# A merged instruction order, with one matmul cadence in the scheduler's clock instead of two

## The chip, the cores and the metric

The kernel runs on one core of a Trainium2 chip. The metric is the device time of one execution in microseconds (us); lower is better. Of several executions the median is given. Engines are named as the profile names them: PE (TensorE, matrix multiply), PEld (its weight loads), DVE (VectorE), ACT (ScalarE), POOL (GpSimd), SP (SyncE, which here issues all DMAs). Each engine takes its instructions strictly in the order in which the program lists them.

## The reference

One decoder layer over 576 tokens: 512 of a prompt and 8 sequences of 8 sample tokens. What is computed, cut to its core:

```
proj = rmsnorm(x, norm1_g) @ w_in                     # -> qkv_a, z, beta, a, q_b, k_b, v_b
qkv_a = silu(short_conv(qkv_a))                       # mixer A: gated DeltaNet, 4 heads of 128
lmat  = strict_lower((kb @ k.T) * decay); a_mat = lmat + I
u, w  = triangular_solve(a_mat, vb), triangular_solve(a_mat, kb * exp(G))
S     = scan over chunks;  oa = rmsnorm(o) * silu(z)
ob    = dilated_mixture(q_b, k_all, v_all)            # mixer B: 8 heads of 64, sample tokens
                                                      # attend to a cache of 1024 past tokens
h1 = x + concat(oa, ob) @ w_o
y  = h1 + square(relu(rmsnorm(h1) @ w_up)) @ w_down   # 1024 -> 4096 -> 1024
```

Outputs are y, the new keys and values, the DeltaNet states and the last convolution rows.

## The kernel before

Tokens stand on the free axis, 576 columns, in two halves of 288. A weight product is made in three matmuls: each factor is split into a high part (type fp32r, by ACT) and a low part (the rest, by DVE or POOL), and high by high, high by low and low by high are summed in PSUM. The stages are: `proj_a` (q, k and v of mixer B; tiles `pa`, 260 or 512 columns a matmul; weight chunks `wq`, `wk`, `wv`), `proj_b` (everything of mixer A; tiles `pg`, 288 columns; chunks `wb`), the prompt's attention in 16 units (`sc`, `ptp`, `pv`), the sample tokens' attention (`s`, `os`, `pts`, `ocT`; its cached keys and values come in 48 DMAs of 512 KB into `kv` and `morekv`), the triangular solve (`sub_prompt`), the DeltaNet chain (`py`, `pu`, `cha`, `chb`, `cs`, `sn`), the output projection `proj_o` (first its attention half, `pg<-mob`, then its DeltaNet half, `pg<-moa`) and the feed-forward stage `mlp_gemm` (2904 matmuls of 288 columns, tiles `pg<-xf` and `pg<-hid`).

No order is written by hand. Each stage is a set of generators ("tasks") that queue their operations; the class `Flow` (L72 on) merges them while the kernel is built. For every engine it keeps a rough clock `free[engine]`; each operation has a cost in ns; at each step the task whose next operation can start soonest (plus a bias of its kind) is issued, and the engine's clock moves on by the cost. Tasks added with `fill=True` (`proj_a`, `proj_b`, `proj_o`, `mlp_gemm`) take PE whenever nothing else is ready on it. So the costs decide, for every engine at once, where an operation that waits for another engine stands among the filling matmuls; nothing of this clock exists when the program runs.

The cost of a matmul is given by `mm` (L257): the number of columns divided by 2.4, plus 3 ns, plus `extra`. The feed-forward stage passes `extra=8` (in `three` and in its call of `gemm`), all others nothing.

Three places matter further on:

- The zero fill (`zero_fill`, L1155): 25 us into the planner's clock POOL sets a tile `zero`, and SP writes it to the scratch `dU` in DRAM: 2064 rows of 129 floats, 1032 KB. Around it stand the loads of the chunks `wk`, which the k group of `proj_a` needs.
- The sums of squares of x: ACT squares (`sq<-xr`), POOL adds (`acc<-acc,sq`, seven times), PE sums over partitions (`ssum`), DVE forms the variance, POOL takes the power (`rs`), and PE broadcasts it (`rowb`).
- The triangular solve: 15 pairs of small steps on DVE (`sub<-sub`), a few DMAs between SBUF places, then eight pairs of a product and a sum (`pr<-sub`, `sub<-pr`), then DMAs through `dU` into `silvz`, on which PE's first product of the chain (`py<-silvz,big`) waits. After the last matmul of `proj_b` PE makes the transposes `pvt`, `pss`, `pk`, `pq`, whose results DVE and ACT take out of PSUM, and what else is ready, up to that `py`.

Of the kernel before, what the change touches and what calls it, by code (L numbers as in the profile page):

```python
# [11 lines left out]
F32R = mybir.dt.float32r  # L12
# [200 lines left out]
def hymba_step(ctx: ExitStack, tc: tile.TileContext, a):  # L213
# [14 lines left out]
    def get(use, shape, name, dt=F32):  # L228
        k = home[use]
        free = lambda: live[use] < cap[use] and live[k] < cap[k]  # L230
        while not free():
            yield free
        live[use] += 1
        live[k] += 1
        return pools[k].tile(shape, dt, name=name, tag=k, bufs=cap[k])

    def rel(*uses):
        def go():
            for u in uses:
                live[u] -= 1  # L240
                live[home[u]] -= 1
        fl.do(go)
# [5 lines left out]
    def size(x):  # L248
        n = 1
        for q in x.shape[1:]:  # L250
            n *= q
        return n
# [1 line left out]
    on_psum = lambda x: x.tensor.space == PSUM  # L254
    ap = lambda x: not isinstance(x, (int, float))

    def mm(out, lhsT, rhs, start, stop, share=1, extra=0):  # L257
        n = size(rhs) * (1 if rhs.dtype == F32R else 4)
        cost = max(n, size(lhsT) * (1 if rhs.dtype == F32R else 4)) / 2.4 + 3 + extra
        cost = cost if share == 1 else cost / share + 15  # L260
        fl.op("PE", (cost, n / share * lhsT.shape[0] / 128),
              lambda: nc.tensor.matmul(out, lhsT, rhs, start=start, stop=stop, skip_group_check=True))  # L262
# [230 lines left out]
    def weights(g, k):  # L493
        if (g, k) not in wready:
            yield lambda: (g, k) in wready
        w, t = wready.pop((g, k))
        fl.at(t + 200)
        return w
# [58 lines left out]
    def warm_up():  # L557


        act(warm, zeros[:, :1])  # L560
        p = yield from get("x", [128, 128], "warm")
        for _ in range(WARM):
            mm(p, zeros, zeros, True, True)
        rel("x", "k")
# [36 lines left out]
    def token_sums(src):  # L601
        p = yield from get("x", [128, 5], "ssum")
        for t, (o, n) in enumerate(TT):
            mm(p[:n, t:t + 1], src[:, o:o + n], ones[:, 0:1], True, True)
        yield 0
        return p
# [396 lines left out]
    sil = {}  # L1003
    UW = 604

    def gemm(wh, wl, x_h, x_l, nk, stride, off, after, extra=0):


        for hf, (c0, c1) in enumerate(HALF):
            p = yield from get("g", [128, 288], "pg")  # L1010
            for j in range(nk):
                s = slice(j * stride + off, j * stride + off + 128)
                mm(p, wh[:, s], x_h[:, j, c0:c1], j == 0, False, extra=extra)
                mm(p, wh[:, s], x_l[:, j, c0:c1], False, False, extra=extra)
                mm(p, wl[:, s], x_h[:, j, c0:c1], False, j == nk - 1, extra=extra)
                yield 0
            fl.spawn(after(hf, p))

# [651 lines left out]
    high = lambda t, j, n=1: t[:, j * 288:(j + n) * 288]  # L1670
    low = lambda t, j, n=1: t[:, (j + 8) * 288:(j + 8 + n) * 288]
# [89 lines left out]
    hid, Q, read = {}, {}, {}  # L1761
# [8 lines left out]
    def three(p, w, c, x, j, first, last):  # L1770
        c = slice(c * 128, c * 128 + 128)
        l = w[:, 512:]
        mm(p, w[:, c], high(x, j), first, False, extra=8)
        mm(p, w[:, c], low(x, j), False, False, extra=8)
        mm(p, l[:, c], high(x, j), False, last, extra=8)

    def up_classical(u):

        fl.spawn(up_square(u))
        w, P = {}, {}  # L1780
        for i in range(4):
            for hf in range(2):
                for r in range(2):
                    if not i:
                        P[hf, r] = yield from get("g", [128, 288], "pg")
                    for k in range(2):
                        if (r, k) not in w:
                            w[r, k] = yield from weights(("u", u), f"A{r + 1}{k + 1}")
                        j = 2 * hf + k
                        yield from factor(("x", i), j)  # L1790
                        three(P[hf, r], w[r, k], i, xf[i], j, i == 0 and k == 0, i == 3 and k == 1)
                        yield 0
        for hf in range(2):
            for r in range(2):
                fl.spawn(up_relu(u, hf, r, P[hf, r]))
        rel("mw", "mw", "mw", "mw")
# [6 lines left out]
    def up(u):  # L1803
        fl.spawn(up_square(u))
        A = yield from get("g", [128, 288], "pg")
        for p in PO:
            w = yield from weights(("u", u), p)
            if p in (2, 5):
                B = yield from get("g", [128, 288], "pg")
            if p in (6, 7, 3, 4):  # L1810
                yield from seen(("u", u, {6: 1, 7: 6, 4: 7, 3: 5}[p]))
            P = B if p in (2, 5, 3) else A
            for i in range(4):
                j = OF_X[p]
                yield from factor(("x", i), j)
                three(P, w, i, xf[i], j, i == 0 and p in (1, 2, 5), i == 3)
                yield 0
            rel("mw")
            fl.spawn(up_out(u, p, P), "out")
# [59 lines left out]
    def add_down(m, hf, p, last):  # L1879
        c0, c1 = HALF[hf]  # L1880
        tt(h1[m][:, c0:c1], p, h1[m][:, c0:c1], OP.add)
        rel("g")
        if last:
            yield 0
            dma(a["yT"][:, m, c0:c1], h1[m][:, c0:c1])
        yield 0

    def mlp_gemm():
        yield lambda: "proj_o" in done
        for g in order:  # L1890
            if g[0] == "d":
                c, i = g[1:]
                wh, wl = yield from weights(g, 0)
                if not i:
                    yield lambda: all(("hid", 2 * c + q, hf) in done for q in range(2) for hf in range(2))
                for j in range(2):
                    after = lambda hf, p, m=2 * i + j: add_down(m, hf, p, c == 7)
                    yield from gemm(wh, wl, hid[c][:, 0], hid[c][:, 1], 4, 256, j * 128, after, extra=8)
                rel("mw", "mw")
                if i == 3:  # L1900
                    rel("big")
                continue
            if g[1] % 2 == 0:
                hid[g[1] // 2] = yield from get("big", [128, 2, 4, NT], "hid", F32R)
            if g[1] < CLASSICAL:
                yield from up_classical(g[1])
            else:
                yield from up(g[1])
            if g == ("u", 15):
                rel("big", "big", "big", "big")  # L1910
# [36 lines left out]
    fl.add(proj_o(), "fill", True)  # L1947
    fl.add(stats2())
    fl.add(mlp_gemm(), "fill", True)
    fl.run()  # L1950

# [89 lines left out]
```

## Time and profile before

| what | value |
|---|---|
| median of 3 runs | 818.16 us (816.64 to 821.53) |
| the profiled execution | 818.95 us, its span 817.2 us |
| PE busy | 792.2 us, 97% of the span |
| DVE busy | 568.7 us, 70% |
| ACT busy | 348.3 us, 43% |
| POOL busy | 109.4 us, 13% |
| feed-forward stage, the last piece of the chain of waits | 370.65 us, 2794 matmuls recorded |

Busy time counts an instruction from its start to its end, and neighbouring matmuls overlap; a PE that starts its matmuls late still reads as busy as long as a gap stays below the length of one matmul (some 290 ns). A timeline row gives the start, the time it covers, the operation as `output<-inputs`, how many were merged, and in brackets how long the engine sat idle before it and what ended that.

### The profile page before, as it was taken

The page shows a single profiled execution, that of the slowest core. Times are in us where ns is not written, and L with a number is a line of the kernel's source. Part 1 is how long each engine was busy: PE and PEld are TensorE (multiplying, and loading weights), DVE is VectorE, ACT ScalarE, POOL GpSimd, SP SyncE. Part 2 cuts the span into 40 slices and gives each one's busy share as a digit, 9 for nine tenths or more (in the row PEclk, how much of TensorE's full clock was granted, in tenths as well). Part 3 has the DMA queues.
Part 4 walks back from the last instruction along what each step waited for, and adds up shares of the span by engine and source line. Part 5 has one row for each costly group of instructions (what it writes and reads, how often), then busy time and mean ns, then how long its engine had stood idle before and what let it go on. Part 6 is the DMA issues. An engine that isn't in the chain of part 4 may idle for free.

```text
span 817.2 us, 15699 instructions
## 1 busy us (share of the span) xinstructions
PE 792.2 (97%) x6323; PEld 728.1 (89%) x6323; DVE 568.7 (70%) x1250; ACT 348.3 (43%) x728; POOL 109.4 (13%) x128
## 2 busy tenths in 40 slices
PE   8989998999999999999997999999999999999998
PEld 8968877879778687778997999999999999999998
DVE  4366269888776785668798886768677676867642
ACT  5547453655242134443466543515343351534400
POOL 3443224134224000121000000000000000000000
PEclk9999999999999999999999999999999999999999
DMA  7732320106686799122221141404123130412302
GB/s 270 125 112 77 123 68 31 55 27 245 211 345 185 273 319 327 49 93 81 104 104 52 59 150 52 129 27 155 53 94 113 52 129 27 155 53 95 112 30 87
DMA packets 49864, 99.05 MB, mean 121 GB/s; under 512 B 12864, under 2 KB 26304, under 8 KB 49792
## 3 DMA queue, kind: packets, MB, share of 16 engines
q1 hardware_dynamic: 49792, 98.05, 36.6%
q8 instruction: 50, 0.82, 0.4%
q14 instruction: 22, 0.18, 0.1%
HBM read 88.15 MB, written 9.69 MB: 120 GB/s over the span
## 4 chain that ended last, share of the span: by engine, by line
PE 73%; issue 9%; DVE 7%; DMA 6%; ACT 2%; SPq 2%; POOL 1%; POOLq 0%; ACTq 0%; DVEq 0%
PE pg L262 53%; PE pa L262 7%; DVE y L285 2%; SPq L321 2%; PE cha L262 2%; DMA wr<-in_wk_dram 2%; DMA morekv<-in_cv_dram 1%; PE os L262 1%; PE ptp L265 1%; DMA morekv<-in_ck_dram 1%; PE cs L262 1%; DMA silvz<-dU 1%; PE sc L262 1%; PE s L262 1%; PE sn L262 1%
## 5 line engine op out<-in xcount | busy, mean ns | idle before, releaser
L262 PE MATMUL pg<-hid,mw 128*128 128x288 f32 x1536 | 204.7, 295 | 0.0
L262 PEld LDWEIGHTS pg<-hid,mw 128*128 128x128 f32 x1536 | 203.9, 188 | 0.0
L262 PE MATMUL pg<-xf,mw 128*128 128x288 f32 x1368 | 186.0, 297 | 4.6 <-ACT xf L270 3.8
L262 PEld LDWEIGHTS pg<-xf,mw 128*128 128x128 f32 x1368 | 183.7, 189 | 5.6 <-ACT xf L270 4.3
L278 DVE TENSOR_TENSOR h<-pg,h 128x288 f32<-128x288 f32 x160 | 72.5, 455 | 94.6 <-PE pg L262 93.8
L270 ACT ACTIVATE mw<-wr 128x512 fp32r<-128x512 f32 (+1 forms) x82 | 62.9, 791 | 70.8 <-PE pg L262 70.1
L262 PE MATMUL pg<-xh,wh 128*128 128x288 f32 x256 | 78.0, 305 | 0.0
L262 PE MATMUL pg<-xl,wh 128*128 128x288 f32 x256 | 78.0, 305 | 0.0
L262 PE MATMUL pg<-xh,wl 128*128 128x288 f32 x256 | 77.9, 304 | 0.0
L278 DVE TENSOR_TENSOR mw<-wr,mw 128x512 fp32r<-128x512 f32 (+1 forms) x82 | 72.4, 893 | 6.7 <-ACT mw L270 6.3
L270 ACT ACTIVATE mw<-ws 128x512 fp32r<-128x512 f32 x56 | 33.7, 627 | 45.3 <-PE pg L262 26.6
L262 PEld LDWEIGHTS pg<-xh,wh 128*128 128x128 f32 x256 | 48.4, 189 | 3.2 <-issue 3.0
L262 PEld LDWEIGHTS pg<-xh,wl 128*128 128x128 f32 x256 | 48.4, 189 | 2.8 <-issue 2.4
L262 PEld LDWEIGHTS pg<-xl,wh 128*128 128x128 f32 x256 | 48.5, 189 | 2.5 <-issue 1.9
L308 POOL TENSOR_TENSOR wl<-wr,wh 128x1024 fp32r<-128x1024 f32 x15 | 35.9, 2393 | 81.6 <-ACT wh L270 65.0
L262 PE MATMUL pa<-wh,xh 128*128 128x260 f32 (+1 forms) x128 | 43.1, 344 | 1.0 <-ACT wh L270 1.0
L262 PE MATMUL pa<-wh,xl 128*128 128x260 f32 (+1 forms) x128 | 43.6, 348 | 0.5 <-DVE xl L285 0.4
L262 PE MATMUL pa<-wl,xh 128*128 128x260 f32 (+1 forms) x128 | 42.7, 341 | 0.0
L270 ACT ACTIVATE wh<-wr 128x1024 fp32r<-128x1024 f32 (+1 forms) x40 | 38.6, 964 | 8.0 <-DMA wr<-in_wk_dram 5.1
L270 ACT ACTIVATE uq<-pg 128x288 f32<-128x288 f32 x42 | 17.1, 408 | 58.0 <-PE pg L262 58.0
L285 DVE SCALAR_TENSOR_TENSOR y<-u,cp,y 128x600 f32<-128x600 f32 x36 | 37.1, 1032 | 5.9 <-ACT u L270 3.3
L278 DVE TENSOR_TENSOR wl<-wr,wh 128x1024 fp32r<-128x1024 f32 (+1 forms) x25 | 28.4, 1134 | 16.0 <-ACT wh L270 15.9
(295 smaller groups left out, 1311.1 us busy)
## 6 DMA issues: line engine op xcount, KB each, us to landing
wr<-in_wu_dram SPq DMA_DIRECT2D x32, 512.0 KB, 3.3
wr<-in_wd_dram SPq DMA_DIRECT2D x32, 512.0 KB, 3.3
morekv<-in_ck_dram SPq DMA_DIRECT2D x20, 512.0 KB, 5.4
morekv<-in_cv_dram SPq DMA_DIRECT2D x20, 512.0 KB, 5.3
wr<-in_wb_dram SPq DMA_DIRECT2D x16, 512.0 KB, 4.0
wr<-in_wo_dram SPq DMA_DIRECT2D x8, 512.0 KB, 6.1
xr<-in_xT_dram SPq DMA_DIRECT2D x8, 288.0 KB, 5.6
h<-in_xT_dram SPq DMA_DIRECT2D x8, 288.0 KB, 7.2
```

Source lines behind the costliest of these rows:

```text
L262: lambda: nc.tensor.matmul(out, lhsT, rhs, start=start, stop=stop, skip_group_check=True))
L265: fl.op("PE", (97, 230), lambda: nc.tensor.transpose(out, in_, ident[:k, :k]))
L270: fl.op("ACT", cost, lambda: nc.scalar.activation(out, in_, func, bias=bias, scale=scale, accum_out=accum), mark)
L278: dve(lambda: nc.vector.tensor_tensor(out, x, y, op=op), out, x, mark=mark)
L285: dve(lambda: nc.vector.scalar_tensor_tensor(out, x, s, y, op0=op0, op1=op1), out, x, 61 if ap(s) else 0, mark=mark)
L308: fl.op("POOL", (135 + size(x) / 0.47) * slow, lambda: nc.gpsimd.tensor_tensor(out, x, y, op=op), mark)
L321: fl.op("SP", 4 * slow * size(dst) * dst.shape[0] / 360.0, lambda: nc.sync.dma_start(dst, src), mark)
```

## The change

The term `extra` goes, and the constant in `mm` rises from 3 to 11.5. A feed-forward matmul of 288 columns is then booked at 131.5 ns (131 before), one of any other stage at 131.5 (123 before), one of 512 columns at 224.8 (216.3 before), one of 260 at 119.8 (111.3 before); small fp32 matmuls also get 8.5 ns more, those that share the array (`share`) a part of it. No computation, tile, buffer count or bias changes; the merge runs anew over all stages and engines.

```diff
-    def mm(out, lhsT, rhs, start, stop, share=1, extra=0):
+    def mm(out, lhsT, rhs, start, stop, share=1):
         n = size(rhs) * (1 if rhs.dtype == F32R else 4)
-        cost = max(n, size(lhsT) * (1 if rhs.dtype == F32R else 4)) / 2.4 + 3 + extra
+        cost = max(n, size(lhsT) * (1 if rhs.dtype == F32R else 4)) / 2.4 + 11.5
...
-    def gemm(wh, wl, x_h, x_l, nk, stride, off, after, extra=0):
+    def gemm(wh, wl, x_h, x_l, nk, stride, off, after):
...
-        mm(p, w[:, c], high(x, j), first, False, extra=8)
+        mm(p, w[:, c], high(x, j), first, False)
...
-                    yield from gemm(wh, wl, hid[c][:, 0], hid[c][:, 1], 4, 256, j * 128, after, extra=8)
+                    yield from gemm(wh, wl, hid[c][:, 0], hid[c][:, 1], 4, 256, j * 128, after)
```

What the new merge moves, at the places that are spoken of below. First the queue of SP near the start of the program, as a difference (`wq`, `wk`: weight chunks; `dU<-zero`: the zero fill):

```order
 L321 DMA wr<-in_wq_dram 128x520 x4
-L321 DMA wr<-in_wk_dram 128x1024
 L321 DMA dU<-zero 2048x1x129
-L321 DMA wr<-in_wk_dram 128x1024 x3
+L321 DMA wr<-in_wk_dram 128x1024 x4
 L321 DMA sU<-zero 128x129
```

The first of the four `wk` loads now stands behind the zero fill instead of ahead of it. The same place on POOL:

```order
 L308 ISA
-L308 TENSOR_TENSOR acc<-acc,sq 128x576 x3
+L308 TENSOR_TENSOR acc<-acc,sq 128x576 x2
 L314 MEMSET zero 128x129
-L308 TENSOR_TENSOR acc<-acc,sq 128x576 x4
+L308 TENSOR_TENSOR acc<-acc,sq 128x576 x5
 L317 TENSOR_TENSOR rs_81<-var_80,neghalf 128x5
```

The tile that the zero fill reads is set one addition earlier. Then DVE at the end of the triangular solve, before:

```order
L278 TENSOR_TENSOR pr<-sub 128x512
L292 TENSOR_REDUCE sub<-pr 128x32
L278 TENSOR_TENSOR pr<-sub 128x512
L282 TENSOR_SCALAR oc<-os,sms 128x64
L292 TENSOR_REDUCE sub<-pr 128x32
L278 TENSOR_TENSOR pr<-sub 128x512
L278 TENSOR_TENSOR big_3442<-pvt,sv 128x4x128
L292 TENSOR_REDUCE sub<-pr 128x32
```

and DVE at the same place now, again up to the eighth and last `sub<-pr` (`big<-pvt` takes PE's transpose `pvt` out of PSUM; `wl` is the low part of a `wo` chunk):

```order
L278 TENSOR_TENSOR wl<-wr,wh 128x1024
L292 TENSOR_REDUCE sub<-pr 128x32
L278 TENSOR_TENSOR big_3528<-pvt,sv 128x4x128
L278 TENSOR_TENSOR pr<-sub 128x512
L278 TENSOR_TENSOR wl<-wr,wh 128x1024
L292 TENSOR_REDUCE sub<-pr 128x32
L278 TENSOR_TENSOR big_3528<-pvt,sv 128x4x128
L278 TENSOR_TENSOR pr<-sub 128x512
L285 SCALAR_TENSOR_TENSOR oc<-os,sms,oc 128x64
L292 TENSOR_REDUCE sub<-pr 128x32
```

The first `big<-pvt` stood ahead of the eighth `sub<-pr` and now stands ahead of the seventh pair, with a `wl` and a second `big<-pvt` between. Last, PE between the end of `proj_b` and the first `py`, its last rows, before:

```order
L265 MATMUL pvt<-c,silvz 128x128 x4
L262 MATMUL os<-morekv,eTs 32x128 x13
L265 MATMUL pss<-c,silqk 64x128
L265 MATMUL pq<-c,silqk 128x128 x4
L265 MATMUL pss<-c,silqk 64x128
L265 MATMUL pss<-c,silvz 64x128
L265 MATMUL pk<-c,silqk 128x128 x4
L262 MATMUL os<-morekv,eTs 32x128 x3
L262 MATMUL os<-kv,eTs 32x128 x8
L262 MATMUL os<-morekv,eTs 32x128 x8
L265 MATMUL pq<-c,silqk 128x128 x4
L262 MATMUL cs<-so,kq 32x128 x5
```

and its last rows now:

```order
L265 MATMUL pvt<-c,silvz 128x128 x3
L265 MATMUL pq<-c,silqk 128x128 x4
L265 MATMUL pvt<-c,silvz 128x128
L265 MATMUL ocT<-c,oc 64x128
L265 MATMUL pk<-c,silqk 128x128 x4
L265 MATMUL pq<-c,silqk 128x128 x4
L265 MATMUL pss<-c,silqk 64x128 x2
L265 MATMUL pss<-c,silvz 64x128
L265 MATMUL pq<-c,silqk 128x128 x4
L262 MATMUL cs<-so,kq 32x128 x16
L262 MATMUL pg<-mob,wh 128x288 x2
L262 MATMUL py<-silvz,big_3527 128x64 x4
```

The 32 `os` products of the sample attention no longer stand in this stretch: they are all ahead of the last matmul of `proj_b`. Two matmuls of the output projection are new in it, and four `pk` transposes have gone behind the first `py`.

## Rows read from the trace of the kernel before

**Rows 1.** The page's first part: busy us, share of the span, instructions, by engine.

```profile
PE 792.2 (97%) x6323; PEld 728.1 (89%) x6323; DVE 568.7 (70%) x1250; ACT 348.3 (43%) x728; POOL 109.4 (13%) x128
```

**Rows 2.** What PE waited for: us in total, times, longest us.

```profile
PE ptp L265 <- DVE e L282: 6.2, 7, 2.4
PE pg L262 <- ACT xf L270: 3.8, 2, 3.1
...
PE os L262 <- DMA morekv<-in_cv_dram: 1.8, 2, 1.1
```

**Rows 3.** Pieces of the chain of waits: start us, us, what and how many.

```profile
87.60 11.78 PE pa L262 x51
99.38 4.08 PE pg L262 x31
...
443.15 370.65 PE pg L262 x2794
```

**Rows 4.** Timeline of SP near the start: start us, us of issuing, what.

```profile
17.02 0.33 SPq L321 DMA_DIRECT2D wr<-in_wk_dram  x1
26.31 0.62 SPq L321 DMA_DIRECT2D dU<-zero  x1
27.03 4.08 SPq L321 DMA_DIRECT2D wr<-in_wk_dram  x3
```

**Rows 5.** Timeline of POOL at the same place.

```profile
22.49 1.42 POOL L308 TENSOR_TENSOR acc<-acc,sq 128x576 f32<-128x576 f32 x1 [1.13 <-ACT sq L270]
...
26.07 0.21 POOL L314 MEMSET zero<- 128x129 f32 x1
```

**Rows 6.** DMA issues of the first 50 us: KB each, us from issue to landing.

```profile
dU<-zero SPq DMA_DIRECT2D x1, 1032.0 KB, 12.6
```

**Rows 7.** Timelines of ACT and of DVE: the second `wk` chunk is split.

```profile
39.53 1.06 ACT L270 ACTIVATE wh<-wr 128x1024 fp32r<-128x1024 f32 x1 [5.08 <-DMA wr<-in_wk_dram]
...
40.62 1.23 DVE L278 TENSOR_TENSOR wl<-wr,wh 128x1024 fp32r<-128x1024 f32 x1 [6.30 <-ACT wh L270]
```

**Rows 8.** Timeline of PE: first matmul of the k group, and its stop.

```profile
34.03 0.39 PE L262 MATMUL pa<-wh,xh 128*128 128x512 f32 x1
...
40.70 0.49 PE L262 MATMUL pa<-wh,xs 128*128 128x512 f32 x1
43.88 0.65 PE L265 MATMUL rowb<-c,rs 128*128 128x128 f32 x4 [2.69 <-POOL rs L317]
```

**Rows 9.** One stretch by engine: its length, busy us (PE, PEld, DVE, ACT, POOL), clock, DMA.

```profile
43.90:48.30 4.40, 4.40 (x14) 3.14 (x15) 3.06 (x10) 1.76 (x3) 3.61 (x3) 0.61 0.53 156
```

**Rows 10.** Timeline of DVE around the end of the triangular solve.

```profile
278.83 1.22 DVE L278 TENSOR_TENSOR wl<-wr,wh 128x1024 fp32r<-128x1024 f32 x1
...
296.67 0.68 DVE L278 TENSOR_TENSOR pr<-sub 128x512 f32<-128x512 f32 x1
297.72 0.69 DVE L278 TENSOR_TENSOR big<-pvt,sv 128x512 f32<-128x512 f32 x1 [0.37 <-PE pvt L265]
298.33 0.68 DVE L292 TENSOR_REDUCE sub<-pr 128x32 f32<-128x512 f32 x1
...
300.03 0.27 DVE L285 SCALAR_TENSOR_TENSOR oc<-os,sms,oc 128x64 f32<-128x64 f32 x1
```

**Rows 11.** Timeline of PE after the last matmul of `proj_b`, to the first `py`.

```profile
297.08 0.60 PE L265 MATMUL pvt<-c,silvz 128*128 128x128 f32 x4
297.52 0.38 PE L265 MATMUL pss<-c,silqk 128*64 128x128 f32 x2
...
308.35 1.08 PE L262 MATMUL py<-silvz,big 128*128 128x64 f32 x8
```

**Rows 12.** Pieces of the chain of waits in the same stretch: the `os` products.

```profile
302.03 0.99 PE os L262 x26
...
304.51 1.22 PE os L262 x38
```

**Rows 13.** SP in this stretch, and the tile `silvz`: DMA to landing us, min/median/max.

```profile
303.82 0.91 SPq L321 DMA_DIRECT2D silvz<-dU  x2
...
DMA to landing us min/median/max: 4.4/5.6/7.2
```

More of the change, by code (lines that the diff above doesn't have):

```diff
@@ L1012, in gemm @@
                 s = slice(j * stride + off, j * stride + off + 128)
-                mm(p, wh[:, s], x_h[:, j, c0:c1], j == 0, False, extra=extra)
-                mm(p, wh[:, s], x_l[:, j, c0:c1], False, False, extra=extra)
-                mm(p, wl[:, s], x_h[:, j, c0:c1], False, j == nk - 1, extra=extra)
+                mm(p, wh[:, s], x_h[:, j, c0:c1], j == 0, False)
+                mm(p, wh[:, s], x_l[:, j, c0:c1], False, False)
+                mm(p, wl[:, s], x_h[:, j, c0:c1], False, j == nk - 1)
                 yield 0
@@ L1772, in three @@
         l = w[:, 512:]
-        mm(p, w[:, c], high(x, j), first, False, extra=8)
-        mm(p, w[:, c], low(x, j), False, False, extra=8)
-        mm(p, l[:, c], high(x, j), False, last, extra=8)
+        mm(p, w[:, c], high(x, j), first, False)
+        mm(p, w[:, c], low(x, j), False, False)
+        mm(p, l[:, c], high(x, j), False, last)
     def up_classical(u):
```

## The prediction

> **What bounds the kernel now.** I read the page's busy times first: PE is busy for 792.2 us, 97% of the span [rows 1], so no other engine sets the end as a whole, and the change adds or takes away no matmul. What it can move is the time in which PE stands, and that lies in the stages before the feed-forward. The chain of waits says so too: from 443.15 us on it is one piece of PE, 2794 matmuls in 370.65 us, 132.7 ns each [rows 3]. That stage is booked at 131 ns before and 131.5 after, so its order hardly has a reason to change, and I take nothing from it. Second, the list of what PE waited for [rows 2]: it is short, some transposes of the attention (6.2 us), the entry into the feed-forward (3.8) and the cache loads (1.8). Third, the timelines at the places where the new order differs most on SP, POOL, DVE and PE.
>
> **Is the new clock truer?** Yes. A 288-column matmul of the projections comes every 131.6 ns (31 in 4.08 us) and one of 512 columns every 231 ns (51 in 11.78 us, with small work between) [rows 3]. The planner had booked 123 and 216; it now books 131.5 and 225. But a truer PE clock means that in the order an instruction that waits for DVE, ACT or a DMA is followed less far behind: the old clock made the filling matmuls look cheaper by 8.5 ns each, put more of them between a producer and its consumer than its own latencies asked for, and so gave slack against every latency that the planner underrates. That slack goes. I count two places where it decides, and leave the rest at zero with bounds.
>
> **Part 1, the start: the first wk chunk behind the zero fill.** Before, SP issues the first wk load at 17.02, the zero fill at 26.31 and the other wk loads from 27.03 on [rows 4]. The fill takes 12.6 us to land [rows 6], and the wk load right behind it reaches ACT at 39.53, 12.5 us after its issue [rows 4, 7]. In the new order all four loads stand behind the fill. The fill is earlier, since POOL sets its tile after the second addition instead of the third: that addition ends at 22.49 + 1.42 = 23.91, the set takes 0.21, so about 24.1 in place of 26.28 [rows 5], and SP's issue follows it by 0.03: 24.15. The first wk load is issued 0.72 later, at 24.9, and by the same 12.5 us it reaches ACT at 37.4. DVE begins its low part 1.09 after ACT began (39.53 to 40.62) and takes 1.23 [rows 7], so the second matmul of the k group can run at 39.7. PE has work up to 34.03, where that group begins [rows 8], and one matmul of it more once the high part is there. So PE stands for 39.7 - 34.0 - 0.2 = **5.5 us**, new. Against it: the 2.69 us stop ahead of rowb [rows 8] has the same cause. There the variance on DVE stood behind the low part of the second wk chunk, which waited for the fill [rows 7]. In the new order PE comes to that rowb late, while the second chunk follows the first closely, so I take this stop away: 5.5 - 2.7 = **+2.8 us**. After the old stop the granted clock was 0.61 over 4.4 us [rows 9], which is a stretch at the lower level (1.2 GHz); PE had been idle before it. After a stop of twice the length I expect it again and count nothing for it. Bounds: 0, if the first chunk overtakes the fill; 5.5, if the old stop stays as well.
>
> The Trainium skill, page "DMA: Bandwidth & Descriptors", section Specifications, puts the smallest transfer that runs at line rate at 512 B and the limit of one core's HBM at about 358 GB/s. The fill's rows are 516 B. By that rule its 1032 KB would be an estimated 3 us of transfer, the wk chunk would be there before 34 us and part 1 would be nil. The row says 12.6 us [rows 6], and the row decides; the rule returns at rival 2.
>
> **Part 2, the end of the triangular solve.** PE's first py waits for a chain: last sub<-pr on DVE, then DMAs through dU, then silvz. Before, the first big<-pvt starts on DVE at 297.72 and the last sub<-pr at 298.33, done at 299.01 [rows 10]; the load of silvz is issued at 303.82 and takes 4.4 us or more [rows 13], and py starts at 308.35 [rows 11]: 9.3 us from the last sum to py, and 4.4 us after the load's issue is 308.2, so py followed the load at once. Between the first pvt (297.08) and that py PE fills 11.3 us with transposes, os and cs [rows 11].
>
> In the new order two things change. (a) DVE makes, between the first big<-pvt and the last sum, one more pr (0.68), one wl (1.22), one sum (0.68), a second big<-pvt (0.69), another pr (0.68) and a small oc (0.27) [rows 10]: 4.2 us by their durations, and since such rows start some 0.08 earlier than their neighbours' ends (297.72 to 298.33 is 0.61 for a row of 0.69), **3.7 us**. All of it is after the first pvt, since engines keep their order, and all of it is ahead of the chain's DMAs. (b) PE has less to do meanwhile: the 32 os products are gone from here, 26 and 38 records, 0.99 + 1.22 = 2.2 us [rows 12]; four pk transposes, 0.44 us by the four pvt (297.08 to 297.52) [rows 11]; three pts of the same kind, 0.3; two projection matmuls come in, 0.27 at 132 ns [rows 3]. Together **2.7 us** less. That work is not saved: it stands further ahead, where PE had no hole for it. So PE stands 3.7 + 2.7 = **+6.4 us** longer. Bounds: 3, if the loads through dU land sooner because the last cache loads are then over (the chain still has its three steps on DVE); 8, if after such a stop the clock stands at its lower level as in [rows 9], 3.4 us at half speed, part of it on PE's path.
>
> **Part 3, everything else.** The transposes ptp of the prompt attention wait 6.2 us for DVE in all [rows 2]. Between a unit's scores and its first transpose the new order has less PE work in nine units and more in six, as read from both orders; I take 0, with -4 to +4. The cache loads cost PE 1.8 us [rows 2]; the same queue on SP stands behind the loads of the solve in both orders: 0, -2 to +2. At the entry into the feed-forward (3.8 us) [rows 2] DVE and ACT are what is late, with the same work: 0, -2 to +2.
>
> **Sum.** 2.8 + 6.4 + 0 = 9.2 us. The profiled execution, 818.95 us with a span of 817.2, lies 0.8 above the median of the runs, 818.16; against that median the sum gives 827.4, and I say **827 us**.
>
> **Rivals.** (1) *Faster: the attention's stops go.* The waits of ptp and os are 8.0 us [rows 2], and where the second kind stood the clock fell too; if a truer clock puts these consumers where they are really ready, up to 8 us go. It decides the sign if it saves more than parts 1 and 2 cost, that is over 9.2 us with my values or over 3 with their low ends (0 and 3). Both at once gives 818.2 + 3 - 8 = 813. For it: the waits exist. Against it: the new order shortens the distances more often than it lengthens them. (2) *No change: the fill does not block and the chain is shorter than I think.* Parts 1 and 2 at their low ends give 818.2 + 3 = 821. For it: the loads differ in size and in what else is queued. Against it: the wk load right behind the fill did take 12.5 us [rows 4, 7], and the chain's steps on DVE can't overlap. By the rule of the Trainium skill's page "DMA: Bandwidth & Descriptors", Specifications, named above, part 1 would take this low end. (3) *Worse than forecast:* the old stop stays beside the new one (+5.5) and part 2 costs 8, with 3 of lost slack at the ptp: 818.2 + 16.5 = 834.7. (4) *The change does nothing,* because a merge by readiness gives nearly the same order: ruled out, since the SP, DVE and PE rows differ at the places above.
>
> **How the numbers follow.** Forecast 0.55 and rival 3 0.10 are slower; rival 2 0.22; rival 1 0.13. A difference below 0.5% (4.1 us, so 814.1 to 822.3) is about what a measurement of this kernel can tell from none. Slower 0.65, same 0.23, faster 0.12. The range runs from 815, between rivals 1 and 2, to 834, just short of rival 3.
>
> **What would show it.** Right: in the new trace ACT's first wh of a wk chunk starts near 37 and PE's second k matmul near 40, with some 5 us idle ahead of it and no stop ahead of rowb; the last sub<-pr ends some 5.6 us after the first pvt begins (1.9 before), and PE sits idle for 5 to 7 us in all up to the first py. The feed-forward piece keeps its 132.7 ns. Wrong: a wk chunk that lands before 34; a py that follows the last sum by much less than 9 us; or waits of ptp that fall from 6 us to under 2.

## The result, and the profile after

The changed kernel takes 850.76 us (median of 4 runs, 839.54 to 851.23), beside 817.4 us for the kernel before (median of 4): a ratio of 1.0366, with a 95% interval of 1.0273 to 1.0458. Forecast were 827.0 us and a range that ended at 834. The direction was right; the size was 33 us where I had worked out 9. The profiled execution took 851.23 us, with a span of 849.1. The runs of the changed kernel differ by more than those of the kernel before, and with them their mean granted clock: 0.960 in the profiled run, 0.974 in the shortest.

The page's first line and its row of the granted clock in 40 slices:

```profile
PE 818.1 (96%) x6323; PEld 749.2 (88%) x6323; DVE 565.3 (67%) x1250; ACT 348.3 (41%) x728; POOL 109.9 (13%) x128
PEclk9899999999999996579999999999999999999999
```

PE was busy for 792.2 us before [rows 1] and is now for 818.1: **25.9 of the 32 us are busy time**, with the same number of matmuls recorded, 6323. A longer list of waits alone can't do that. The row of the clock says where to look: three slices in a row with 6, 5 and 7 tenths, from 318 to 382 us; there is an 8 in the second slice, too.

The stretches between the same program points, before and after: start and end, length, busy us (records) of PE, PEld, DVE, ACT and POOL, granted clock, DMA share, GB/s. The points are the first and the last `pa`, the first `pvt`, the first `py`, the first `pg<-moa`, the first `pg<-xf`, and the end of the last `rowb`, in the entry into the feed-forward. Before:

```profile
5.67:98.99 93.32, 89.99 (x517) 76.54 (x518) 48.88 (x91) 52.40 (x95) 37.35 (x38) 0.98 0.48 134
98.99:297.08 198.09, 188.08 (x1820) 157.19 (x1819) 154.35 (x450) 79.78 (x184) 54.94 (x67) 0.99 0.51 174
297.08:308.35 11.27, 11.02 (x158) 9.13 (x157) 8.97 (x24) 8.80 (x44) 0.00 (x0) 1.00 0.90 278
308.35:393.09 84.74, 83.94 (x703) 67.88 (x703) 57.80 (x140) 32.89 (x107) 14.62 (x10) 1.00 0.42 146
393.09:418.53 25.44, 25.44 (x195) 25.44 (x193) 21.12 (x43) 14.22 (x26) 0.00 (x0) 1.00 0.25 93
418.53:443.08 24.55, 19.33 (x127) 17.94 (x125) 22.82 (x51) 16.57 (x35) 1.55 (x1) 0.93 0.12 44
```

After:

```profile
5.86:103.39 97.53, 92.30 (x517) 78.27 (x518) 48.50 (x91) 52.49 (x95) 37.50 (x38) 0.95 0.44 129
103.39:309.78 206.39, 195.66 (x1937) 162.08 (x1936) 153.84 (x455) 82.65 (x188) 55.74 (x67) 0.98 0.53 182
309.78:323.01 13.23, 7.95 (x89) 6.76 (x88) 11.89 (x27) 8.03 (x39) 0.59 (x1) 1.00 0.71 238
323.01:426.16 103.15, 102.52 (x655) 84.35 (x656) 51.96 (x131) 30.80 (x109) 13.60 (x10) 0.77 0.26 91
426.16:451.60 25.44, 25.44 (x194) 25.44 (x193) 21.95 (x45) 15.07 (x28) 0.00 (x0) 1.00 0.19 63
451.60:474.60 23.00, 18.90 (x124) 17.56 (x122) 21.59 (x48) 15.26 (x33) 1.55 (x1) 0.93 0.15 50
```

Length less busy time is how long PE sat idle. So the account reads:

| stretch | longer by | of it PE idle | of it PE busy |
|---|---|---|---|
| `proj_a` | +4.2 | +1.9 | +2.3 |
| `proj_b` and the attentions | +8.3 | +0.7 | +7.6 |
| last transposes, up to `py` | +2.0 | +5.0 | -3.1 |
| chain and first half of `proj_o` | +18.4 | -0.2 | +18.6 |
| second half of `proj_o` | 0 | 0 | 0 |
| entry into the feed-forward | -1.6 | -1.1 | -0.4 |
| sum | +31.3 | +6.4 | +25.0 |

The idle time, which is all that the prediction summed, is 6.4 us. The busy time comes in two lots. In `proj_b` most of the 7.6 us is work that only stands elsewhere now (117 more records there, 69 and 48 fewer in the two stretches behind, whose share is 3.1 and, as the first experiment will show, 2.8 us). The other 1.7 us are what one more stretch of 3.41 us at the lower clock would cost, an estimate: such stretches begin at 213.84 and 271.87 after, and only at 270.17 before. In the chain the records are fewer and the busy time is longer. Split where the granted clock comes back, that stretch reads:

```profile
323.01:370.86 47.85, 47.85 (x239) 38.97 (x240) 12.80 (x34) 9.98 (x39) 4.37 (x3) 0.50 0.21 67
370.86:426.16 55.30, 54.67 (x417) 45.38 (x417) 39.16 (x97) 20.81 (x70) 9.23 (x7) 1.00 0.31 111
```

From the first `py` on the granted clock is 0.50, the lower level of 1.2 GHz, for 47.85 us on end, with PE busy all the time. Before, the stretch that answers to it ran at 1.00 throughout. This is what to explain.

The front has its own, smaller one. The stretch at the lower clock that goes with the stop there, before and after:

```profile
44.89:48.30 3.41, 3.41 (x9) 2.24 (x8) 2.10 (x5) 1.45 (x3) 3.41 (x3) 0.50 0.68 202
36.35:46.59 10.24, 8.11 (x23) 6.33 (x24) 6.96 (x17) 6.82 (x15) 4.09 (x3) 0.50 0.62 233
```

What PE waited for, after (us in all, times, longest):

```profile
PE pa L262 <- ACT wh L270: 4.4, 2, 3.8
PE ocT L265 <- DVE oc L285: 3.5, 2, 2.5
PE pg L262 <- ACT xf L270: 3.1, 1, 3.1
PE ptp L265 <- DVE e L282: 2.8, 4, 1.2
PE sb L262 <- DVE silqk L285: 2.6, 2, 2.4
PE pk L265 <- DVE big L278: 1.9, 1, 1.9
PE py L262 <- DMA silvz<-dU: 1.8, 1, 1.8
```

Against [rows 2]: `ptp` went from 6.2 to 2.8, and waits of `ocT`, `sb`, `pk` and `py` have come. The stop of `rowb` (2.7 before) has gone, and one of `pa` has come.

The place of the prediction's part 1, in the timelines of SP, ACT and PE (start us, us, what, and in brackets the idle time before it):

```profile
24.13 0.62 SPq L321 DMA_DIRECT2D dU<-zero  x1
24.81 6.35 SPq L321 DMA_DIRECT2D wr<-in_wk_dram  x4
...
36.91 1.06 ACT L270 ACTIVATE wh<-wr 128x1024 fp32r<-128x1024 f32 x1 [4.79 <-DMA wr<-in_wk_dram]
...
38.02 0.79 PE L262 MATMUL pa<-wh,xh 128*128 128x512 f32 x1 [3.77 <-ACT wh L270]
39.28 0.79 PE L262 MATMUL pa<-wl,xh 128*128 128x512 f32 x1 [0.47 <-DVE wl L278]
```

The place of part 2, in the timelines of DVE, SP and PE: the first product of a `pvt`, the last sum, the load of `silvz`, and three stops, the last ahead of `py`:

```profile
310.93 0.68 DVE L278 TENSOR_TENSOR big<-pvt,sv 128x512 f32<-128x512 f32 x1
...
315.25 0.67 DVE L292 TENSOR_REDUCE sub<-pr 128x32 f32<-128x512 f32 x1
...
318.88 0.91 SPq L321 DMA_DIRECT2D silvz<-dU  x2
...
314.59 0.66 PE L265 MATMUL pk<-c,silqk 128*128 128x128 f32 x4 [1.93 <-DVE big L278]
...
317.18 0.27 PE L265 MATMUL ocT<-c,oc 128*64 128x128 f32 x1 [1.06 <-DVE oc L285]
...
323.01 1.88 PE L262 MATMUL py<-silvz,big 128*128 128x64 f32 x8 [1.77 <-DMA silvz<-dU]
```

### The profile page after: what moved, and what is told of

The parts are those of the page before. It is cut to its first block, busy times and chain, and to the rows that moved or that the text cites. A ratio compares the mean times of both kernels' runs of the same rounds, so it can differ in the third digit from the quotient of the medians.

```text
span 849.1 us, 15707 instructions
## 1 busy us (share of the span) xinstructions
PE 818.1 (96%) x6323; PEld 749.2 (88%) x6323; DVE 565.3 (67%) x1250; ACT 348.3 (41%) x728; POOL 109.9 (13%) x128
## 4 chain that ended last, share of the span: by engine, by line
PE 73%; issue 12%; DVE 7%; DMA 3%; POOL 2%; ACT 2%; SPq 0%; POOLq 0%; ACTq 0%; DVEq 0%
PE pg L262 51%; PE pa L262 7%; PE cha L262 2%; DVE y L285 2%; DMA wr<-in_wk_dram 1%; PE py L262 1%; PE sn L262 1%; PE pu L262 1%; PE cs L262 1%; PE ptp L265 1%; PE sc L262 1%; POOL wl L308 1%; PE chb L262 1%; PE os L262 1%; PE s L262 1%
## 5 line engine op out<-in xcount | busy, mean ns | idle before, releaser
L285 DVE SCALAR_TENSOR_TENSOR y<-u,cp,y 128x600 f32<-128x600 f32 x36 | 39.0, 1084 | 6.9 <-ACT y L270 5.4
```

What stands on the lines that cost most here:

```text
L285: dve(lambda: nc.vector.scalar_tensor_tensor(out, x, s, y, op0=op0, op1=op1), out, x, 61 if ap(s) else 0, mark=mark)
```

## The experiments

**A filled stop.** The first question is whether the 18 us of the chain come from the clock or from the chain's new order, in which the matmuls of `proj_o` are mixed in. The edit puts matmuls that nobody reads right ahead of the first `py`, in its own PSUM tile; the planner books nothing for them, so the order of all else stays.

```diff
+                if c == 0 and not filled:
+                    filled.append(1)
+                    ahead(py.rearrange("p c n -> p (c n)")[:, :128], 7)   # 7 matmuls of ident by ident
                 mm(py[m, c], L[h][r, c, m], blk(Uh[r, c], 1), True, True)
```

> The changed kernel with seven matmuls of 128 columns (about 0.23 us each, 1.6 us) put on PE right ahead of the first py, in the same tile and with no time booked for them, so that the order of all else is that of the changed kernel. PE does useless work there instead of waiting 1.8 us for silvz. Theory A (the 18 us between the first py and the end of the first output projection are lost to the granted clock, which was at its lower level for 47.8 us from 323.07 on, and the stop ahead of py let it fall): although work is added, the time falls to 832 (829 to 836), the stretch from the first py to the last pu takes 25 us as before instead of 53, at granted clock 1.00. Theory B (the new order of the chain itself is thin, the clock only follows): 850 to 852, granted clock near 0.5 there as in the changed kernel.

Measured: 829.25 us (828.08 to 830.27), 1.0132 of the kernel before (1.0104 to 1.0160). Seven useless matmuls (the profile records each twice) save 21.5 us. PE's timeline at the place:

```profile
321.15 1.72 PE L269 MATMUL py<-c 128*128 128x128 f32 x14
323.32 1.07 PE L266 MATMUL py<-silvz,big 128*128 128x64 f32 x8 [0.44 <-DMA silvz<-dU]
```

And the stretch from `py` to the first `pg<-moa`, with the columns of the stretches above:

```profile
323.32:405.28 81.96, 81.18 (x655) 67.11 (x656) 51.50 (x131) 30.59 (x108) 13.38 (x10) 1.00 0.32 112
```

The same order, with 655 records in both, takes 81.96 us at clock 1.00 and 103.15 at 0.77. Theory A holds for this place. The new order of the chain is no worse than the old one: its busy time of 81.18 us is 2.8 less than before (83.94), with 48 records fewer, which now stand further ahead.

The Trainium skill, page "TensorE: Matmul & The Clock Gate", section "HAM oscillation — how this bites in real kernels", prices such a penalty as the time at the lower level times one half. By that, 47.85 us would cost an estimated 23.9 us; the two rows show 21.2, so the trace nearly agrees.

**A stop in the order before.** If a stop does it, the kernel before must show it too. One run delays the solve on DVE, by products that are done again ahead of its last sum; two doses.

```diff
+                if out is u12 and k == 6:
+                    again = (pr, x[:, k:k + 2, None, :]..., y[:, None, :, :]...)
+                    fl.cur.pre = lambda: [nc.vector.tensor_tensor(*again, op=OP.mult) for _ in range(8)]   # or 4
                 red(out[:, k:k + 2], pr)
```

> The kernel before, in its own order, with eight more products of 0.68 us on DVE (5.4 us) between the last two steps of the triangular solve, so that dU, silvz and the first py come 5.4 us later and PE stops there. Theory A: the granted clock falls to the lower level for most of the chain of py, pt and pu, which takes some 50 us instead of 25; with the stop itself 817 + 5.4 + 15 to 20 = 837 to 843. Theory B (the order, not the stop): only the stop is paid, with at most 1.7 us for one short stretch at the lower level as after the stops of the kernel before: 822 to 825.

> The same with four more products (2.7 us). Theory A gives one of two values with little between: 820 if a stop of 2.7 us, with the 0.7 that was there, does not let the clock fall, or some 835 if it does; the dose alone would be 820. Theory B: 820 to 822.

Measured: 824.02 us with eight (1.0070; 1.0048 to 1.0092) and 820.5 with four (1.0039; 1.0015 to 1.0063). That is theory B's number: the stop was paid and little else, in each of eight and ten runs (none above 826.6). Theory A as I had put it, any stop here will do, has fallen. What differs is seen in PE's timeline with eight:

```profile
305.12 0.39 PE L273 MATMUL ocT<-c,oc 128*64 128x128 f32 x1 [5.95 <-DVE oc L293]
```

And in the stretch at the lower clock of the same run:

```profile
302.41:309.24 6.83, 4.12 (x37) 3.73 (x38) 5.78 (x16) 2.49 (x14) 0.00 (x0) 0.50 0.47 102
```

PE's queue stood still for 5.95 us, and the clock fell. But the queue stood at an `ocT`, ahead of the last transposes and of the `os` products. These ran for 9.5 us before the first `py`, which came at 314.64, and the clock was back at 309.24.

**The same stop, further behind.** So the theory needs the place: a fall just where the chain begins. This run delays only the DMAs, through one more DRAM tile, so that PE stands right ahead of `py`.

```diff
-            dma(dap(dU, ...), u12[r], "dU", 2.5)
+            nc.sync.dma_start(mid, u12[r])     # mid: rows of a new DRAM tile dV
+            nc.sync.dma_start(dap(dU, ...), mid)
```

> The kernel before, in its own order, with the last two loads of the solved blocks into dU made in two steps each, through one more DRAM tile, so that silvz and the first py come some 4 to 5 us later, while no engine other than SP has more to do. PE then stops right ahead of the first py, after the transposes, and not in front of them as with the longer solve on DVE. Theory A2 (what costs is a fall of the granted clock just where the chain of py, pt and pu begins, since that chain does not bring the clock back): granted clock 0.5 through most of the chain, 25 us become some 45, in all 817.5 + 4.5 + 18 = 840. Rival (the chain in the order of the kernel before, with the os products in it, brings the clock back by itself): 817.5 + 4.5 + 2 = 824.

Measured: 842.28 us (median of four runs: 826.97 at a mean clock of 0.990, and 839.19, 845.36 and 847.88 at 0.957 to 0.969). The stop in PE's timeline:

```profile
311.34 1.94 PE L266 MATMUL py<-silvz,big 128*128 128x64 f32 x8 [5.78 <-DMA silvz<-dU]
```

The stretch at the lower clock:

```profile
308.38:352.76 44.38, 41.42 (x263) 33.55 (x264) 12.38 (x34) 9.96 (x29) 1.50 (x2) 0.50 0.47 155
```

A stop of 5.78 us, in the order of the kernel before, was followed by 44.38 us at the lower level; nearly the same stop (5.95), 9.5 us of PE's work ahead of that `py`, by 6.83. The order before is thus not immune: in its own profile PE comes to `py` without a stop [rows 11], and the longest one in the chain is 0.74 us. Nor does it need the added delay: of the eight runs of the kernel before that were taken beside these, one took 837.05 us at a mean clock of 0.967, which by an estimate from that mean is 55 us at the lower level in all, where the profiled run has 11. One run of the four with the delay escaped. Why a run falls or escapes is open.

**Work put into the chain.** Does the level stay low because of what PE does in the chain, or for a time of its own? The edit of the first run again, but ahead of the third `py`, behind the fall, and 14 of them.

> The changed kernel, its stops left as they are, with fourteen matmuls of 128 columns (0.25 us each at the full clock, 3.4 us; 6.9 at half) put ahead of the third py, some 8 us behind the point where the granted clock fell. Theory A2 (the lower level stays because the work of the chain, short and dependent, does not bring the clock back): a few us of dense work bring it back, the lower stretch ends near 340 instead of 370.9, which saves some 12 to 15 us of the 18; with the 5 us of work added the time is 838 to 843. Rival (once lowered, the level stays for a time of its own, whatever PE does): the lower stretch stays near 48 us and the time rises to 856.

Measured: 834.68 us (833.17 to 837.57), 1.0207 (1.0173 to 1.0241): 16 us less than the changed kernel, with work added and every stop left in place. The stretches from the first `pvt` to `py`, from there to the end of the lower level, and on to `pg<-moa`:

```profile
309.37:322.70 13.33, 7.95 (x90) 6.76 (x88) 11.98 (x27) 8.28 (x39) 0.59 (x1) 1.00 0.73 246
322.70:332.82 10.12, 10.12 (x49) 10.12 (x50) 2.58 (x8) 2.45 (x9) 2.46 (x2) 0.50 0.85 267
332.82:412.67 79.85, 79.08 (x636) 64.97 (x636) 49.02 (x123) 28.33 (x100) 11.15 (x8) 1.00 0.23 84
```

The fillers start at 331.37, and the lower stretch ends at 332.82, after 10.12 us instead of 47.85. So it does not last for a time of its own: it ends within a block of 128-column matmuls, where the chain's mixture of short products and transposes had left it as it was. One profile could owe that to chance; the mean clocks speak for all runs. Estimated from them, PE stood at the lower level for 20 to 28 us in all in each of these four runs, and for 44 to 68 us in the four of the changed kernel. (The 44 are its shortest run: there the stretch must have ended sooner without a block.) PE counts as busy all the time in both (10.12 of 10.12 us here), so this can't be read from its busy time.

**The front.** In the changed kernel the zero fill is issued behind the first `wk` load instead of ahead of it; nothing else changes places.

```diff
-        dma(dap(dU, ...), z[:, None, :].to_broadcast([128, 16, 129]))
+        held.append(lambda: nc.sync.dma_start(dap(dU, ...), z...))   # issued right behind the first wk load
```

> The changed kernel with one DMA moved: the zero fill of dU is issued right behind the first wk load instead of ahead of it, all else in the order of the changed kernel. My prediction's part 1 says that the stop ahead of the second k matmul (3.8 us, and the stretch at the lower clock after it) comes from that one transfer: no stop there, the last pa 4.4 us earlier, at 99, and the time 850.8 - 4.4 = 846.4 if the chain's long stretch at the lower clock stays, 828 if that goes with it. Rival (the wk load is late for another reason, for example its own place in the queue): the stop stays, 851.

Measured: 828.87 us (median of 7 runs, 821.37 to 843.71). In its profiled run, the shortest, the waits of `pa` for `wh` are gone, and the front (first to last `pa`, columns as above) reads

```profile
5.69:96.83 91.14, 89.84 (x517) 76.96 (x518) 48.11 (x91) 52.52 (x95) 38.25 (x38) 1.00 0.47 137
```

that is 6.4 us less than in the changed kernel: 3.9 of idle time (97.53 - 92.30 against 91.14 - 89.84) and 2.5 of busy time, at clock 1.00 instead of 0.95. Part 1's cause was right: the first `wk` load, issued at 21.02 instead of 24.81 as SP no longer holds it until POOL has set the tile, landed 3.1 us after its issue, where behind the fill ACT began 12.1 us after it. The chain's long stretch is not in this profile, though the stops ahead of `py` are all there. Here the clock fell earlier, among the transposes, and was back before `py` came at 314.64:

```profile
306.75:310.16 3.41, 3.31 (x17) 2.94 (x16) 3.27 (x10) 0.92 (x4) 0.00 (x0) 0.50 0.19 28
```

The runs near 840, with mean clocks of 0.965 to 0.973, can hardly be without it. Estimated from the mean clocks, the seven runs stood at the lower level for 11 to 59 us in all, with values between. So the length of the stretch changes from run to run in the same order, and I can't say on what that hangs.

**All stops that I knew.** The late fill, the fillers ahead of `py`, and more of them at `sb`, `pk` and two `ocT`.

> The changed kernel with the zero fill behind the first wk load and with matmuls that nobody reads in five of its stops: nine ahead of the sb that waits for silqk, nine and four ahead of the two ocT that wait for oc, seven ahead of the pk that waits for DVE, seven ahead of the first py; 0.25 us each, all else in the order of the changed kernel. If the 32 us are the front's stop (4.4), the stretch at the lower clock from py on (18.4) and the short stretches at the lower clock after the other stops (1.7 each), 850.8 - 4.4 - 18.4 - 2 x 1.7 - 2 (the front's own lower clock) = 822 to 825, in all of its runs. If the stops themselves cost and not the clock after them: 846, as for the late fill alone at its worst.

Measured: 824.11 us (five runs, 822.18 to 827.45), 1.0082 (1.0054 to 1.0110). In the profiled run the lower level does not occur before the entry into the feed-forward (there it lasts 13.65 us, from 434.04 on), and no run is near 840. That is the number forecast. It is still 6 us above the kernel before. PE's idle time, 21.2 us (821.9 - 800.7), is less than there (25.0), but the 36 fillers are themselves some 9 us of work, an estimate at 0.25 us each, and the stretch in the entry was 3.41 us before. Two things went otherwise than meant: the nine at an `ocT` stand ahead of the one after the one that waits, so that they are pure cost (2.2 us), and those at `pk` had to wait as `pk` had, since what `pk` waits for is its PSUM tile, which DVE's `big<-pvt` or `big<-pk` gives back.

**One part of the booking alone.** The new constant for the matmuls of the projections only, and for the small matmuls only; then 7 ns for both.

```diff
-        cost = max(...) / 2.4 + 11.5
+        cost = max(...) / 2.4 + (11.5 if fl.cur.fill else 3)                       # projections only
+        cost = max(...) / 2.4 + ((11 if <feed-forward> else 3) if fl.cur.fill else 11.5)   # small ones only
+        cost = max(...) / 2.4 + (11 if <feed-forward> else 7)                      # half way
```

> The new booking for the matmuls of the projections alone, the small matmuls of the attentions, the solve and the chain booked as in the kernel before. Read from its order: the zero fill stands ahead of the first wk load as in the changed kernel, but the os products stand in the end of the solve, ahead of py, as in the kernel before. By my account the front costs 4.4 and the clock stays up in the chain: 817.5 + 4.4 = 822 (819 to 825). Rival (each new order brings its own stops, and the account of the places is luck): anything from 815 to 850, with stops at other places.

> The new booking for the small matmuls alone, the projections booked as in the kernel before. Read from its order: the first wk load stands ahead of the zero fill and the os products stand in the end of the solve, both as in the kernel before. By my account neither price is paid: 817.5 (814 to 821). Rival (it is the booking of the small matmuls that makes the chain's order thin, with or without a stop): 835 to 850.

> The booking half way: 7 ns beside the columns for every matmul outside the feed-forward, in place of 3 before and 11.5 after. Read from its order: the zero fill stands ahead of the first wk load, as in the changed kernel, and the os products stand ahead of py, as in the kernel before. By the account of the places: the front's price (4 to 6) and some new stops of the attention (0 to 5), but no long stretch at the lower clock in the chain: 822 to 829. Rival (the loss grows with the number booked, half of it at half way): 834.

Measured: 828.29 us (1.0138; 1.0112 to 1.0164), 832.57 (1.0183; 1.0158 to 1.0208) and 832.77 (1.0154; 1.0103 to 1.0205, runs from 826.65 to 842.24). In the profiles of all three the chain runs at clock 1.00, as expected where the `os` products stand ahead of `py`; the longest run half way, at a mean clock of 0.972, can hardly have done so. None of the three medians is at the number that I had for it; the second is 15 us off, and the third is near its rival's 834. What PE waited for in the second gives half of the reason:

```profile
PE ptp L265 <- DVE e L282: 11.2, 7, 2.7
PE pg L262 <- ACT xf L270: 3.8, 2, 3.1
PE ocT L265 <- DVE oc L285: 2.3, 1, 2.3
PE sb L262 <- DVE silqk L285: 2.3, 1, 2.3
PE rowb L265 <- POOL rs L317: 2.2, 1, 2.2
```

It has neither of the two prices, and 5.0 us more at `ptp`, and 2.0 and 1.7 more at `ocT` and `sb`. From the order I had looked at two places; the others had moved as well. By the pages, span less PE's busy time is 25.0 us before, 27.2 with the projections alone, 30.7 with the small ones, 28.0 half way and 31.0 after (829.1 - 801.9, 828.5 - 797.8, 827.1 - 799.1, 849.1 - 818.1). Every one of these orders makes PE wait longer than the order before. But that is the smaller part of the loss: PE's busy time is 9.7, 5.6 and 6.9 us longer than before. With the projections alone most of the 9.7 is the clock, at the lower level for 10.24 us in the front and for 13.65 in the entry into the feed-forward (3.41 each before; half of what is added is an estimated 8.5 us). The entry is a place that I had not counted:

```profile
440.94:454.59 13.65, 12.58 (x50) 11.51 (x51) 10.08 (x25) 7.06 (x15) 1.61 (x1) 0.50 0.22 77
```

Half way it is 6.83 and 10.24 us. With the small ones alone the clock accounts for under 2 of the 5.6 us; where the rest comes from was not traced. Whether the loss grows with the number booked the half-way run does not settle.

**The kernel before with its stops filled.** The kernel before, with the zero fill behind the second `wk` load and fillers in three stops.

```diff
+                if u == 6 and h + j == 0: ahead(pt[:, 0], 6)          # prompt attention
+                if c == 0 and not filled: ahead(py..., 3)             # first py
+                if not u and i == 3 and j + r == 0:                   # entry into the feed-forward: adds zero
+                    fl.cur.pre = lambda q=P[hf, r], x=f(high(xf[2], 0)): [nc.tensor.matmul(q, zz, x, ...) for _ in range(5)]
```

> The kernel before, with what the runs so far point to: the zero fill of dU issued behind the second wk load instead of behind the first, and matmuls that nobody reads in three of its stops: six of 128 columns ahead of the transpose that waits 2.4 us for DVE near 139, three ahead of the first py, and five of 288 columns with weights of zero ahead of the matmul that waits 3.1 us for the last xf at the entry into the feed-forward. If a stop costs itself and a short stretch at the lower clock after it (3.4 us, so 1.7), then 2.7 + 1.7 at the front and 1.7 each at the two others: 817.6 - 4 to 8 = 810 to 814, faster than both kernels. Rival (the short stretches are not set off by these stops, or the fillers only move the stops): 816 to 819.

Measured: 815.59 us (six runs, 812.75 to 817.62), beside 818.27: a ratio of 0.9968, 0.9938 to 0.9997. A gain of 0.3%, just clear of none, and short of the 810 to 814 that I had expected. Three of the six runs do lie at 812.75 to 813.98, at mean clocks of 0.998 to 1.000; the other three at 817.2 to 817.62, at 0.994, and the profiled run is one of these. PE's timeline at the filled transpose and at the entry:

```profile
136.67 1.90 PE L269 MATMUL ptp<-c 128*128 128x128 f32 x12 [1.85 <-DVE E L293]
...
427.91 2.59 PE L1814 MATMUL pg<-xf,zz 128*128 128x288 f32 x10
431.16 0.40 PE L266 MATMUL pg<-xf,mw 128*128 128x288 f32 x1 [0.66 <-ACT xf L278]
```

And the front:

```profile
5.66:94.49 88.83, 88.19 (x517) 75.71 (x518) 49.29 (x91) 52.21 (x95) 37.49 (x38) 1.00 0.49 142
```

The front takes 4.5 us less (88.83 for 93.32), as worked out. But 2.6 of them go again behind it, in `proj_b` and the attentions (200.69 us for 198.09). The filler at `ptp` is part of it: it needs the PSUM tile of an earlier product, which DVE gives back late, so that it waited for 1.85 us and then stood in the way of the transposes; and the clock fell there for 3.41 us, from 137.84 on, as it does not in the profile of the kernel before. The one in the entry took the place of the wait, which is 0.66 us now, but made nothing shorter: the clock falls there as before (from 438.21 on), and the stretch takes 24.73 us for 24.55.

```profile
416.67:441.40 24.73, 21.83 (x137) 19.50 (x135) 24.16 (x54) 16.52 (x35) 1.55 (x1) 0.94 0.13 49
```

## Why the prediction was right or wrong

**The stops** were read well. Part 1: the fill was issued at 24.13 (24.15 worked out) and the loads at 24.81 (24.9), ACT began at 36.91 (37.4), the matmul on the low part at 39.28 (39.7), and the stop was 3.77 + 0.47 = 4.2 us instead of 5.5, since the low part came 0.4 us sooner, PE had work up to 34.25, and the group's first matmul took 0.79 us at the lower clock where I had counted 0.2. The stop of `rowb` went, as said. Part 2: the last sum ended at 315.92, 6.1 us after the first `pvt` (5.6 worked out); the work that left was 3.1 us by PE's busy time (2.7); PE sat idle 5.0 us longer instead of 6.4, since `py` came 7.1 us after the last sum and not 9.3. That was the reason given for the low bound: SP issued the load of `silvz` 3.0 us after the sum, 4.8 before. Part 3: the waits of the attention changed places, `ptp` 3.4 us less and `os` 1.5 less, `sb`, `ocT` and `pts` more, and the idle time of that stretch grew by 0.7. That is 0 within its bounds; rival 1 had the falling half of it right and did not see the rising half. Together: 6.4 us of idle time measured, 9.2 forecast.

**The clock** is the step that failed, in two sentences. In part 1, "After a stop of twice the length I expect it again and count nothing for it": the lower level lasted 10.24 us there instead of 3.41, and PE's busy time in the front grew by 2.3 us. In part 2, the high bound took "3.4 us at half speed" for a fall of the clock: it lasted 47.8 us and cost 21.2 us, more than all the other terms together. Both sizes came from [rows 9], where projection matmuls of 512 columns followed the stop. I had taken the length of the stretch for a property of the stop. The runs show that in the chain it hangs on what follows the stop. In the profiles it is 6.83 us with transposes and `os` products behind the stop, 44 to 48 with the chain, and 10 with the chain and a block of 128-column matmuls in it. For the front this is no answer: projection matmuls of 512 columns followed its stop before and after, and with nearly the same stop the lower stretch there was 10.24 us in the changed kernel (3.8 us of stop) and 6.83 with work in the chain (3.9). What sets its length there stays open; that it goes with the stop is shown by the late fill. I had read the order that follows `py` only for stops, and had not asked what a slower clock would do to it.

**The moved work** was told rightly ("it stands further ahead, where PE had no hole for it") but seen too small: besides the 3.1 us from the end of the solve, 2.8 us of the chain's work moved ahead as well. By the orders it is what left the stop ahead of `py` bare; no run puts the `os` products alone back.

**The reason for the direction**, slack that goes with the dearer booking of PE, fits the three partial bookings, all slower and all with more idle time, but no run singles it out as the cause; that a planner's truer clock must lose is not shown either, only that none of the four truer ones here found an order as good as the old one. One thing I had not looked at: besides the cost told of above, the planner has a half rate for PE (`Flow.clock`, which books columns / 1.2 behind a stretch that it holds to be thin). So it has a place for the very term that measured 21.2 us here; whether the new constant moved that booking was not tested.

The rivals: 1 and 2 are out, and 3 (834.7) was the nearest, with its stops too many and its clock too small. Of the signs named in advance, ACT near 37, the second k matmul near 40, no stop ahead of `rowb`, the last sum 5.6 us behind `pvt` (6.1) and 5 to 7 us of idle time (5.3) all came. Two of the signs of being wrong came half way: `py` followed the sum by 7.1 us and not 9.3, and the waits of `ptp` fell to 2.8. As forecast, the feed-forward is unchanged (371.0 us from the last `rowb` to the last `pg<-hid`, 370.6 before). What should have stood among them is the row of the granted clock.

## What to carry to other kernels

In this kernel a stop of PE was priced by what followed it: ahead of transposes and wide matmuls it cost itself and 1 to 3 us more, ahead of a chain of small dependent products it could cost several times its length, because the granted clock fell and the chain did not bring it back. The clock fell there in most runs and not in all, so such an order has to be timed in several runs. When an order moves, look first at what stands between the last wide work and the first small product, and if PE must wait there, let it do useless matmuls in a tile that is already free; seven of them saved 21 us here. A filler elsewhere can be worth nothing, as in the entry into the feed-forward. And of two profiles compare PE's busy time before its waits: where it grows with the same instructions, look at the granted clock first.

## What the chip showed that I had not expected

With PE busy for 47.85 of 47.85 us, as the profile counts it, the granted clock stayed at 0.50 through the chain; where a block of 128-column matmuls was put into the chain, it was back at 1.00 1.5 us after the block began (331.37 to 332.82). The same program (the late fill) took 821.4 us in one run and 843.7 in another, at mean clocks of 0.993 and 0.965; what decides it was not found.
